# A decoder trunk on one core: other filling rates in both attentions, a later high part in the FFN, quarters for four weights, and other first and last instructions

## The chip, the cores and the metric

One core of a Trainium2 chip. The metric is device microseconds of one execution. The profile is of one execution on the same core; its times count from the span's start. A tile is [partitions, elements], 128 partitions at most.

## What is computed

A trunk of two layers on 256 tokens, width 1024, all in float32:

```python
# layer 0 (A): h = rmsnorm(x); q, k, v = h @ w_qkv_a; rope on 16 of 64 dims; 16 heads, causal (one block of 256)
x = x + attention(q, k, v) @ w_o_a
x = x + conv_ffn(rmsnorm(x))          # width 2816
# layer 1 (B): k, v = rmsnorm(x) @ w_kv_b (4 heads); q = rmsnorm(x) @ w_q_b (16 heads); rope
# window 128, a learned sink per head in the softmax
x = x + swa_sink_attention(q, k, v, sinks) @ w_o_b
x = x + conv_ffn(rmsnorm(x))
out = rmsnorm(x)

def conv_ffn(h):
    u = h @ w_up                                   # [256, 5632]
    u = conv_b + sum(conv_w[j] * shifted(u, j))    # causal, 3 taps
    gate, val = split(u)
    return (silu(gate) * val) @ w_down
```

## The kernel before

**Numbers.** Each operand of a projection is split into a high and a low part (a value rounded to the matmul's fp32r type, and the rest), and a product is three matmuls: high x high, high x low, low x high. Weights come by DMA in units of 128 x 2048 (`fetch`, three raw tiles), ScalarE makes the high part (`wh`, line 157), VectorE the low part (`wl`, line 160). `prepare` (line 166) does that in halves of 1024 columns or, for the units that line 170 lists, in quarters of 512, each piece a step of a chain. Units 0 to 15 are V, Q, K and output weights of layer A, 16 to 37 the up-projection of FFN 0, 38 to 48 its down-projection, 49 and 50 K and V of B (`U_KV`), 51 to 54 its Q (`U_QB`), 55 to 58 its output weights (`U_OB`), then FFN 1.

**The order of work.** The program is written as one stream for TensorE. `tick(ns)` moves a clock of the planner by the nominal time of the matmuls just issued; `chain(key, (delay, step), ...)` queues steps of the other engines, each due its delay after the one before, and the tick that passes a due time issues the step. `require(key)` issues what is left of a chain at once. So the delays set where an instruction stands in its engine's queue, and each engine does its queue in order.

**Projections and rotation.** `qk_group(g)` projects four heads of Q and K for both blocks of 128 tokens. `rotate` (line 371) then copies the result from PSUM, applies the rope (`rope`, lines 346 to 352, VectorE) and transposes (`to_feature`, line 358, TensorE; copies in line 364 on VectorE and 369 on ScalarE). For the first group both blocks are projected in turn and rotated at the end; behind it on TensorE come the second group's matmuls.

**Attention** (line 378) goes over four groups of four heads: scores of group g+1 (lines 402 to 409; two tiles in PSUM tag "u", one in "acc" or "t"), softmax (masks in line 422 on VectorE, exponentials in 432 on ScalarE, norms in 441 to 450), transposition of the probabilities (`probs_T`, line 461: TensorE in 463, copies to SBUF in 469 on ScalarE and 471 on VectorE), then `values` of group g (line 486), whose output gets its high part in line 492 (ScalarE) and its low part in 493 (VectorE). Between these, `fill(ns)` issues matmuls of a filler for the given nominal time: the projections of the next groups and, at the end, the output projection (`Down`, lines 533 to 538). `lead` is the time filled ahead of the first scores; `rate` gives three times for a group: ahead of its first and its second transposition, and ahead of the next scores. PSUM has four banks of tag "acc", two of "t" and two of "u".

**FFN** (line 608): for each of 22 units of 256 columns, 48 matmuls (lines 627 to 629) into a bank of "t" or "u" in turn, then `post` (line 639): ScalarE's scaled copy of both halves (L660), VectorE's two taps of each half (L664, L666), the gate's Silu on ScalarE (L670), the product on GpSimd (L671), and the high (L675, ScalarE) and low part (L676, VectorE) of the product h. `tail` (line 1002) ends the last 256 columns: sums of squares, the root on GpSimd, scaling and two output transfers.

## Time and profile before

| what | value |
| --- | --- |
| median of 3 runs | 578.2 us (578.08 to 578.53) |
| the profiled execution | 578.59 us, its span 576.7 us |
| TensorE busy | 561.9 us, 97% of the span |
| VectorE busy | 429.2 us, 74% |
| ScalarE busy | 379.3 us, 66% |
| GpSimd busy | 106.3 us, 18% |
| TensorE's granted clock | full, but for the span's last slice |

A line of the profile names the line of the kernel, the engine (PE is TensorE, PEld its weight loads, DVE VectorE, ACT ScalarE, POOL GpSimd, SP the queue of most transfers), the operation and the tiles out<-in. In a timeline the number in square brackets is the engine's idle time just before the instruction, and what ended it. Matmuls overlap at their ends, so the distance of two starts is what a matmul costs; its duration is longer.

### The profile page before, as it was taken

The page shows a single profiled execution, that of the slowest core. Times are in us where ns is not written, and L with a number is a line of the kernel's source. Part 1 is how long each engine was busy: PE and PEld are TensorE (multiplying, and loading weights), DVE is VectorE, ACT ScalarE, POOL GpSimd, SP SyncE. Part 2 cuts the span into 40 slices and gives each one's busy share as a digit, 9 for nine tenths or more (in the row PEclk, how much of TensorE's full clock was granted, in tenths as well). Part 3 has the DMA queues.
Part 4 walks back from the last instruction along what each step waited for, and adds up shares of the span by engine and source line. Part 5 has one row for each costly group of instructions (what it writes and reads, how often), then busy time and mean ns, then how long its engine had stood idle before and what let it go on. Part 6 is the DMA issues. An engine that isn't in the chain of part 4 may idle for free.

```text
span 576.7 us, 10181 instructions
## 1 busy us (share of the span) xinstructions
PE 561.9 (97%) x3858; PEld 505.3 (88%) x3858; DVE 429.2 (74%) x921; ACT 379.3 (66%) x760; POOL 106.3 (18%) x124
## 2 busy tenths in 40 slices
PE   9999999999999999999999999899999999999995
PEld 7878888789999999988888987779999999988884
DVE  6698778589967777677569798779986776777714
ACT  6888777478666566566459698867655656656513
POOL 7231001011222322321002100001222232232003
PEclk9999999999999999999999999999999999999998
DMA  8964434432654454547843633232555445355701
GB/s 331 369 251 159 147 146 147 156 138 74 223 198 165 164 202 145 194 172 288 295 145 112 255 106 114 86 135 74 156 211 194 171 157 209 147 184 218 292 0 73
DMA packets 15455, 100.99 MB, mean 175 GB/s; under 512 B 1968, under 2 KB 2096, under 8 KB 3888
## 3 DMA queue, kind: packets, MB, share of 16 engines
q1 hardware_dynamic: 15120, 100.09, 48.5%
q8 instruction: 30, 0.49, 0.3%
q10 hardware_dynamic: 288, 0.26, 0.1%
q14 instruction: 17, 0.14, 0.1%
HBM read 99.30 MB, written 1.05 MB: 174 GB/s over the span
## 4 chain that ended last, share of the span: by engine, by line
PE 60%; DVE 12%; ACT 12%; POOL 6%; issue 5%; DMA 4%; POOLq 0%; SPq 0%; DVEq 0%; ACTq 0%
PE acc L533 9%; PE acc L534 9%; PE acc L538 9%; POOL m L671 5%; DVE m L666 4%; ACT m L660 3%; DVE m L664 3%; PE acc L317 3%; PE acc L318 3%; PE acc L319 3%; DMA wr<-in_w 3%; PE t L627 3%; PE t L628 3%; PE t L629 2%; DVE wl L160 2%
## 5 line engine op out<-in xcount | busy, mean ns | idle before, releaser
L160 DVE TENSOR_TENSOR wl<-wr,wh 128x1024 fp32r<-128x1024 f32 (+1 forms) x200 | 219.2, 1114 | 32.2 <-ACT wh L157 30.3
L157 ACT ACTIVATE wh<-wr 128x1024 fp32r<-128x1024 f32 (+1 forms) x200 | 188.8, 975 | 31.2 <-PE acc L538 19.8
L671 POOL TENSOR_TENSOR m<-m,m 128x256 f32<-128x256 f32 x44 | 66.4, 1510 | 206.7 <-DVE m L666 179.8
L533 PE MATMUL acc<-wh,q 128*128 128x512 f32 x238 | 94.4, 397 | 3.1 <-ACT q L492 3.1
L534 PE MATMUL acc<-wl,q 128*128 128x512 f32 x238 | 92.9, 390 | 0.0
L627 PE MATMUL u<-q,wh 128*128 128x256 f32 x320 | 88.6, 277 | 0.7 <-DVE m L666 0.7
L628 PE MATMUL u<-q,wh 128*128 128x256 f32 x320 | 88.8, 278 | 0.0
L629 PE MATMUL u<-q,wl 128*128 128x256 f32 x320 | 88.1, 275 | 0.0
L627 PE MATMUL t<-q,wh 128*128 128x256 f32 x288 | 79.6, 276 | 0.7 <-DVE m L666 0.7
L628 PE MATMUL t<-q,wh 128*128 128x256 f32 x288 | 79.3, 275 | 0.0
L629 PE MATMUL t<-q,wl 128*128 128x256 f32 x288 | 79.2, 275 | 0.0
L538 PE MATMUL acc<-wh,q 128*128 128x512 f32 x238 | 77.2, 390 | 0.0
L675 ACT ACTIVATE q<-m 128x256 fp32r<-128x256 f32 x44 | 18.4, 418 | 85.9 <-POOL m L671 85.9
L627 PEld LDWEIGHTS u<-q,wh 128*128 128x128 f32 x320 | 60.1, 188 | 1.3 <-ACT wh L157 1.0
L628 PEld LDWEIGHTS u<-q,wh 128*128 128x128 f32 x320 | 60.1, 188 | 0.1
L629 PEld LDWEIGHTS u<-q,wl 128*128 128x128 f32 x320 | 60.1, 188 | 0.0
L317 PE MATMUL acc<-wh,q 128*128 128x512 f32 (+1 forms) x160 | 57.0, 356 | 0.0
L533 PEld LDWEIGHTS acc<-wh,q 128*128 128x128 f32 x238 | 44.7, 188 | 12.6 <-ACT q L492 3.9
L318 PE MATMUL acc<-wl,q 128*128 128x512 f32 (+1 forms) x160 | 55.6, 347 | 0.0
L319 PE MATMUL acc<-wh,q 128*128 128x512 f32 (+1 forms) x160 | 55.4, 346 | 0.0
L627 PEld LDWEIGHTS t<-q,wh 128*128 128x128 f32 x288 | 54.1, 188 | 1.2 <-ACT wh L157 0.5
L628 PEld LDWEIGHTS t<-q,wh 128*128 128x128 f32 x288 | 54.1, 188 | 0.0
(166 smaller groups left out, 1036.7 us busy)
## 6 DMA issues: line engine op xcount, KB each, us to landing
wr<-in_w SPq DMA_DIRECT2D x90, 1024.0 KB, 4.8
first<-in_xw SPq DMA_DIRECT2D x5, 384.0 KB, 5.5
xr<-in_x SPq DMA_DIRECT2D x2, 512.0 KB, 8.2
first<-in_xw SPq DMA_DIRECT2D x1, 768.0 KB, 7.0
out<-m SPq DMA_DIRECT2D x3, 256.0 KB, 2.1
fin_t<-in_fin SPq DMA_DIRECT2D x1, 512.0 KB, 5.6
first<-in_xw SPq DMA_DIRECT2D x1, 388.0 KB, 3.5
out<-m ACTq DMA_DIRECT2D x1, 256.0 KB, 2.1
```

The lines of the kernel that those rows point to most:

```text
L157: nc.scalar.activation(wq[i][0][:, c], raws[i][:, c], AF.Copy)
L160: nc.vector.tensor_tensor(out=wq[i][1][:, c], in0=raws[i][:, c], in1=f(wq[i][0][:, c]), op=ALU.subtract)
L317: nc.tensor.matmul(o, xh[:, blk(b)], wh, start=(c == 0), stop=False)
L318: nc.tensor.matmul(o, xh[:, blk(b)], wl, start=False, stop=False)
L319: nc.tensor.matmul(o, xl[:, blk(b)], wh, start=False, stop=(c == KC - 1))
L533: nc.tensor.matmul(o, ph[:, blk(b)], hi[:, s_], start=first, stop=False)
L534: nc.tensor.matmul(o, ph[:, blk(b)], lo[:, s_], start=False, stop=False)
L538: nc.tensor.matmul(o, pl[:, blk(b)], hi[:, s_], start=False, stop=end)
L627: nc.tensor.matmul(o, hi[:, s_], xh, start=(c == 0), stop=False)
L628: nc.tensor.matmul(o, hi[:, s_], xl, start=False, stop=False)
L629: nc.tensor.matmul(o, lo[:, s_], xh, start=False, stop=(c == KC - 1))
L671: nc.gpsimd.tensor_tensor(out=h, in0=gs, in1=t[1], op=ALU.mult)
```

## The change

It changes numbers that place instructions, and a few instructions:

- FFN: L675 is due 3400 ns after the gating product instead of 1200.
- Rotation of the first group: the rope is due 450 ns after the copy instead of 750, which puts it behind two quarters of a weight's low part instead of three; its transpositions stand three matmuls earlier on TensorE.
- Attention A: smaller filling times in the last group. Attention B: lead 3500 instead of 5500, and filling times by group.
- The weights of units 52 to 55 are made in quarters.
- The transposed probabilities take PSUM tag "u" instead of "t".
- Start: the copy of g moves from VectorE to GpSimd, two memsets of `kd` stand earlier on GpSimd.
- End: block 0 goes out in one transfer of 128x1024 instead of two; one product on GpSimd and one scaling of 256 columns on VectorE go, a fused product of 256 becomes one of 512; the order there is written out by hand.

```diff
--- before.py
+++ after.py
@@ -167,7 +167,7 @@
 
         if i >= N_UNITS:
             return
-        n = 4 if i <= 5 or 1 <= i - U_UP0 <= 3 or 1 <= i - U_UP1 <= 3 else 2
+        n = 4 if i <= 5 or 1 <= i - U_UP0 <= 3 or 1 <= i - U_UP1 <= 3 or U_QB + 1 <= i <= U_OB else 2
         cut = [slice(k * UNIT // n, (k + 1) * UNIT // n) for k in range(n)]
         w_time[0] = max(clock[0] + 200.0, w_time[0] + 4500.0)
 
@@ -368,11 +368,11 @@
 
         chain(key, (200.0, lambda: nc.scalar.activation(hb, v, AF.Copy)), (600.0, low))
 
-    def rotate(o, n, b, hi, lo, key, copy, then=None):
+    def rotate(o, n, b, hi, lo, key, copy, then=None, wait=750.0):
 
         t = mid()[:, :n * P]
         chain(key, (150.0, lambda: copy(t)),
-              (750.0, lambda: rope(t.rearrange("p (h d) -> p h d", d=HD), 2 * n, b)),
+              (wait, lambda: rope(t.rearrange("p (h d) -> p h d", d=HD), 2 * n, b)),
               (1000.0, lambda: to_feature(t, n, b, hi, lo, key, then)))
 
     def attention(qk, ready, filler, lead, rate, msk, vcol, sink):
@@ -458,7 +458,7 @@
             require("sm", j)
             out_ = []
             for e in range(2):
-                tp = bank("t")
+                tp = bank("u")
                 for i in range(3):
                     nc.tensor.transpose(tp[:, i * P:(i + 1) * P], pr[e][:, i * P:(i + 1) * P], ident)
                 tick(330)
@@ -672,7 +672,7 @@
 
             steps = [(200.0, scale), (700.0, tap2)] if i < n_raw else [(200.0, tap2)]
             chain(("p", i), *steps, (400.0, taps), (1600.0, gate),
-                  (1200.0, lambda: nc.scalar.activation(hi, h, AF.Copy)),
+                  (3400.0, lambda: nc.scalar.activation(hi, h, AF.Copy)),
                   (450.0, lambda: nc.vector.tensor_tensor(out=lo, in0=h, in1=f(hi), op=ALU.subtract)))
             parts.append((hi, lo))
 
@@ -747,10 +747,15 @@
         hi_part(i, c)
         lo_part(i, c)
 
+    kd = [one.tile([P, 2, 2, S], F32R, name=f"kd{i}") for i in range(2)]
+    for t in kd:
+        nc.gpsimd.memset(f(t), 0.0)
+
 
     invf = rb[:, 144:152]
     for j in range(HALF):
         nc.gpsimd.memset(invf[:, j:j + 1], float(THETA ** (-2.0 * j / ROT)))
+    nc.gpsimd.tensor_copy(g1, g0)
     pos_f = rb[:, 152:154]
     nc.gpsimd.tensor_copy(pos_f, pos_i)
     tri = rb[:, :80].rearrange("p (k b d) -> p k b d", k=5, b=NB)
@@ -775,7 +780,6 @@
         wh, wl = (t[:, (c % 4) * 512:(c % 4 + 1) * 512] for t in wq[c // 4])
         if c == 0:
             nc.vector.tensor_copy(wh, raw)
-            nc.vector.tensor_copy(g1, g0)
         nc.scalar.activation(hi, src, AF.Copy, scale=g)
         if c > 0:
             nc.scalar.activation(wh, raw, AF.Copy)
@@ -836,10 +840,6 @@
     used(0)
     used(1)
 
-    kd = [one.tile([P, 2, 2, S], F32R, name=f"kd{i}") for i in range(2)]
-    for t in kd:
-        nc.gpsimd.memset(f(t), 0.0)
-
     def spread(g, src, w):
 
         for e in range(2):
@@ -874,7 +874,7 @@
 
         def finish(b):
             rotate(o[b], 4, b, hi, lo, ("qk", g), lambda t: qk_out(t, b, o[b]),
-                   None if b else lambda src, w: spread(g, src[:, 2:4], w))
+                   None if b else lambda src, w: spread(g, src[:, 2:4], w), 750.0 if g else 450.0)
 
         gens = [proj(o[b], hT, b, cols512(u), (u, u + 1) if b else ()) for b in range(NB)]
         if g == 0:
@@ -905,7 +905,7 @@
     def ready_a(oT):
         o_down.append(Down(U_OA, 4, oT, lambda i: require("o", i)))
 
-    attention(qk, ready_a, filler_a(), 8000.0, lambda g: (7000.0, 3500.0, 2000.0) if g < 3 else (5500.0, 2500.0, 1800.0), mask, lambda h: h, False)
+    attention(qk, ready_a, filler_a(), 8000.0, lambda g: (7000.0, 3500.0, 2000.0) if g < 3 else (4500.0, 2000.0, 1500.0), mask, lambda h: h, False)
     nc.gpsimd.affine_select(out=mask[:, :P], in_=mask[:, :P], compare_op=ALU.is_gt, fill=NEG, base=0,
                             pattern=[[1, P]], channel_multiplier=-1)
 
@@ -969,7 +969,7 @@
     def ready_b(oT):
         o_down.append(Down(U_OB, 4, oT, lambda i: require("o", i)))
 
-    attention(qk, ready_b, filler_b(), 5500.0, lambda g: (3200.0, 2000.0, 1300.0), mask, lambda h: 2 * (h // 8) + h % 2, True)
+    attention(qk, ready_b, filler_b(), 3500.0, lambda g: ((4200.0, 2200.0, 1400.0), (3200.0, 1800.0, 1200.0), (3200.0, 1800.0, 1200.0), (4000.0, 1800.0, 1500.0))[g], mask, lambda h: 2 * (h // 8) + h % 2, True)
 
     hT = new_hT()
     y = [quad(F32, "y") for _ in range(2)]
@@ -994,10 +994,10 @@
         times_fin(b, half(n))
         if b == 0 and n == 1:
             r = rstd_of(b)
+            ot = spaced(qd, D, F32, "q", "ot", 15)
             for m in range(2):
-                ot = mid()
-                nc.scalar.activation(ot, xf[b][:, half(m)], AF.Copy, scale=r)
-                nc.sync.dma_start(out[:P, half(m)], ot)
+                nc.scalar.activation(ot[:, half(m)], xf[b][:, half(m)], AF.Copy, scale=r)
+            nc.sync.dma_start(out[:P], ot)
 
     def tail(m, o):
 
@@ -1009,22 +1009,24 @@
         nc.vector.tensor_tensor(out=x_, in0=o, in1=x_, op=ALU.add)
         if m == 0:
             yo.extend(mid() for _ in range(2))
-            nc.scalar.activation(yo[1][:, S:], x_, AF.Square, accum_out=st[:, 2:3])
+            nc.scalar.activation(yo[0][:, S:], x_, AF.Square, accum_out=st[:, 2:3])
             nc.scalar.activation(st[:, 1:2], st[:, 2:3], AF.Identity, scale=1.0 / D, bias=st[:, 1:2])
-            times_fin(1, c)
             return
-        nc.vector.tensor_tensor_reduce(out=xf[1][:, c], in0=x_, in1=x_, scale=1.0, scalar=0.0,
+        end = ExitStack()
+        end.enter_context(tc.manual_schedule(engines={mybir.EngineType.Activation, mybir.EngineType.DVE}))
+        nc.vector.tensor_tensor_reduce(out=yo[0][:, :S], in0=x_, in1=x_, scale=1.0, scalar=0.0,
                                        op0=ALU.mult, op1=ALU.add, accum_out=st[:, 3:4])
         nc.vector.scalar_tensor_tensor(out=st[:, 0:1], in0=st[:, 3:4], scalar=1.0 / D, in1=st[:, 1:2], op0=ALU.mult,
                                        op1=ALU.add)
         nc.gpsimd.tensor_tensor(out=r_t, in0=st[:, 0:1], in1=mhalf, op=ALU.pow)
         rows = out[P:2 * P]
+        nc.scalar.activation(yo[0][:, :S], xf[1][:, :S], AF.Copy, scale=r_t)
         nc.vector.tensor_scalar(out=yo[0][:, S:], in0=xf[1][:, S:2 * S], scalar1=r_t, scalar2=None, op0=ALU.mult)
-        nc.scalar.activation(yo[0][:, :S], xf[1][:, :S], AF.Copy, scale=r_t)
-        nc.vector.tensor_scalar(out=yo[1][:, :S], in0=xf[1][:, 2 * S:3 * S], scalar1=r_t, scalar2=None, op0=ALU.mult)
+        nc.vector.scalar_tensor_tensor(out=yo[1], in0=xr[1][:, half(1)], scalar=r_t, in1=fin_t[:, half(1)], op0=ALU.mult,
+                                       op1=ALU.mult)
         nc.scalar.dma_start(rows[:, half(0)], yo[0])
-        nc.vector.scalar_tensor_tensor(out=yo[1][:, S:], in0=x_, scalar=r_t, in1=fin_t[:, c], op0=ALU.mult, op1=ALU.mult)
         nc.sync.dma_start(rows[:, half(1)], yo[1])
+        end.close()
 
     r_t = one.tile([P, 1], F32, name="r_t")
     yo = []
```

**First place: ScalarE in the FFN.** `m` and `q` are tiles of `post`, `t` and `u` PSUM banks. Before:

```order
222 L670 ACTIVATE m_250_2353<-m_248_2351 128x256
223 L157 ACTIVATE wh_2431<-wr_2267 128x1024
224 L675 ACTIVATE q_2283<-m_251_2354 128x256
225 L660 ACTIVATE m_253_2422<-t_2355,cp 128x256
226 L660 ACTIVATE m_254_2423<-t_2355,cp 128x256
227 L157 ACTIVATE wh_2431<-wr_2267 128x1024
228 L670 ACTIVATE m_255_2424<-m_253_2422 128x256
229 L157 ACTIVATE wh_2502<-wr_2339 128x1024
230 L675 ACTIVATE q_2283<-m_256_2425 128x256
```

and now:

```order
220 L670 ACTIVATE m_250_2351<-m_248_2349 128x256
221 L157 ACTIVATE wh_2429<-wr_2266 128x1024
222 L660 ACTIVATE m_253_2420<-t_2353,cp 128x256
223 L660 ACTIVATE m_254_2421<-t_2353,cp 128x256
224 L675 ACTIVATE q_2281<-m_251_2352 128x256
225 L157 ACTIVATE wh_2429<-wr_2266 128x1024
226 L670 ACTIVATE m_255_2422<-m_253_2420 128x256
227 L157 ACTIVATE wh_2500<-wr_2338 128x1024
228 L660 ACTIVATE m_259_2492<-u_2425,cp 128x256
```

L675 of a unit (the tile `m_251`, say) stood ahead of both L660 of the next unit (`m_253`, `m_254`); now it stands behind them. The two weight halves (L157) keep their places beside L670.

**Second place: TensorE at the end of attention A.** `t` of L486 is the bank of the last values, `q_1245` and `q_1231` the tile made from it, `acc` the output projection. Before:

```order
478 L533 MATMUL acc_1021<-wh_980,q_1123 128x512
479 L534 MATMUL acc_1021<-wl_981,q_1123 128x512
480 L538 MATMUL acc_1020<-wh_980,q_1123 128x512
481 L538 MATMUL acc_1021<-wh_980,q_1123 128x512
482 L486 MATMUL t_1235<-m_123_1184,v_101 64x256
...
489 L486 MATMUL t_1235<-m_129_1219,v_102 64x128
490 L533 MATMUL acc_1018<-wh_1032,q_1245 128x512
491 L534 MATMUL acc_1018<-wl_1033,q_1245 128x512
492 L533 MATMUL acc_1020<-wh_1032,q_1245 128x512
```

and now:

```order
468 L538 MATMUL acc_1020<-wh_980,q_1123 128x512
469 L538 MATMUL acc_1021<-wh_980,q_1123 128x512
470 L486 MATMUL t_1221<-m_123_1184,v_101 64x256
...
477 L486 MATMUL t_1221<-m_129_1212,v_102 64x128
478 L533 MATMUL acc_1018<-wh_980,q_1123 128x512
479 L534 MATMUL acc_1018<-wl_981,q_1123 128x512
...
488 L538 MATMUL acc_1020<-wh_980,q_1123 128x512
489 L538 MATMUL acc_1021<-wh_980,q_1123 128x512
490 L533 MATMUL acc_1018<-wh_1032,q_1231 128x512
```

Before, the unit that reads the values' tile (`wh_1032`) came right behind the values; now 12 matmuls of the unit before it (`wh_980`) lie between.

**Third place: ScalarE in attention B, ahead of the high part of the third group's values (L492).** Before:

```order
401 L469 ACTIVATE m_422_4247<-t_4242 128x384
402 L157 ACTIVATE wh_4309<-wr_3957 128x512 x4
403 L432 ACTIVATE m_426_4279,hst_4281<-m_426_4279,hst_4281 128x128
404 L432 ACTIVATE m_427_4280,hst_4281<-m_427_4280,hst_4281 128x128
405 L432 ACTIVATE m_426_4279,hst_4281<-m_426_4279,hst_4281 128x256
406 L435 ACTIVATE hst_4281<-hst_4281,sink_t 128x2
407 L432 ACTIVATE m_427_4280,hst_4281<-m_427_4280,hst_4281 128x256
408 L492 ACTIVATE q_4300<-t_4285 128x512
```

and now:

```order
399 L157 ACTIVATE wh_4220<-wr_3874 128x1024
400 L469 ACTIVATE m_422_4256<-u_4251 128x384
401 L432 ACTIVATE m_426_4289,hst_4291<-m_426_4289,hst_4291 128x128
402 L432 ACTIVATE m_427_4290,hst_4291<-m_427_4290,hst_4291 128x128
403 L432 ACTIVATE m_429_4292,hst_4294<-m_429_4292,hst_4294 128x128
404 L432 ACTIVATE m_430_4293,hst_4294<-m_430_4293,hst_4294 128x128
405 L432 ACTIVATE m_426_4289,hst_4291<-m_426_4289,hst_4291 128x256
406 L435 ACTIVATE hst_4291<-hst_4291,sink_t 128x2
407 L432 ACTIVATE m_427_4290,hst_4291<-m_427_4290,hst_4291 128x256
408 L492 ACTIVATE q_4310<-t_4295 128x512
```

Four weight quarters stood ahead of the exponentials; now they are placed one by one behind L492.

## Rows read from the trace of the kernel before

**Rows 1.** The page: busy time of each engine with its share of the span; and from the costliest groups (count, busy us and mean ns, then idle time ahead of them and what ended it) the line of L675.

```profile
PE 561.9 (97%) x3858; PEld 505.3 (88%) x3858; DVE 429.2 (74%) x921; ACT 379.3 (66%) x760; POOL 106.3 (18%) x124
...
L675 ACT ACTIVATE q<-m 128x256 fp32r<-128x256 f32 x44 | 18.4, 418 | 85.9 <-POOL m L671 85.9
```

**Rows 2.** Windows of five stages: start and end, length, then busy us (and instructions) of each engine, TensorE's clock, the share of the DMA engines and GB/s.

```profile
60.00:110.00 50.00, 50.00 (x287) 40.83 (x287) 33.98 (x101) 35.49 (x87) 2.65 (x5) 1.00 0.44 153
...
200.00:250.00 50.00, 49.31 (x395) 47.51 (x395) 36.59 (x57) 29.21 (x48) 14.02 (x9) 1.00 0.49 173
...
300.00:320.00 20.00, 19.34 (x108) 16.17 (x108) 19.89 (x51) 18.62 (x46) 5.67 (x6) 1.00 0.40 138
320.00:370.00 50.00, 48.35 (x381) 42.02 (x379) 40.85 (x163) 41.63 (x120) 0.00 (x0) 1.00 0.38 135
370.00:400.00 30.00, 28.30 (x193) 24.60 (x194) 23.38 (x65) 21.47 (x59) 1.73 (x2) 1.00 0.31 107
```

**Rows 3.** Waits of TensorE: who waited for whom, us in total, times, longest.

```profile
PE acc L533 <- ACT q L492: 3.1, 3, 1.6
PE t L358 <- DVE m L352: 1.4, 3, 0.6
...
PE u L627 <- DVE m L666: 0.7, 2, 0.3
PE t L627 <- DVE m L666: 0.7, 2, 0.3
```

**Rows 4.** TensorE's timeline in FFN 0: the first matmul of a unit and of the next one (start, us, instruction).

```profile
213.31 0.28 PE L627 MATMUL t<-q,wh 128*128 128x256 f32 x1
...
218.75 0.28 PE L627 MATMUL u<-q,wh 128*128 128x256 f32 x1
```

**Rows 5.** The chain that ended last, in FFN 0: start, us, what. One turn of the ring.

```profile
224.31 1.57 POOL m L671
...
225.91 0.42 ACT q L675
226.32 0.92 ACT m L660 x2
...
227.27 0.49 DVE m L664
...
227.79 0.48 DVE m L666
...
229.71 0.48 DVE m L666
...
230.35 1.57 POOL m L671
```

**Rows 6.** Groups by line and shape: the low part of a weight, by its two widths, and the low part of h.

```profile
L160 DVE TENSOR_TENSOR wl<-wr,wh 128x1024 fp32r<-128x1024 f32 x160 | 193.2, 1221 | 23.7 <-ACT wh L157 23.4
...
L160 DVE TENSOR_TENSOR wl<-wr,wh 128x512 fp32r<-128x512 f32 x40 | 26.1, 685 | 8.4 <-ACT wh L157 7.0 <-PE acc L319 1.5
...
L676 DVE TENSOR_TENSOR q<-m,q 128x256 fp32r<-128x256 f32 x44 | 18.8, 428 | 43.4 <-ACT q L675 43.4
```

**Rows 7.** The first rotation: VectorE's timeline, then TensorE's.

```profile
27.57 1.30 DVE L160 TENSOR_TENSOR wl<-wr,wh 128x512 fp32r<-128x512 f32 x2 [1.48 <-PE acc L319]
29.76 0.69 DVE L160 TENSOR_TENSOR wl<-wr,wh 128x512 fp32r<-128x512 f32 x1 [0.90 <-ACT wh L157]
30.37 0.28 DVE L346 TENSOR_TENSOR rb<-m,cs 128x128 f32<-128x128 f32 x1
...
30.58 0.39 PE L319 MATMUL acc<-wh,q 128*128 128x512 f32 x1
31.40 0.63 PE L358 MATMUL t<-ident,m 128*128 128x128 f32 x4 [0.43 <-DVE m L352]
32.32 0.63 PE L358 MATMUL t<-ident,m 128*128 128x128 f32 x4 [0.30 <-DVE m L352]
```

**Rows 8.** The end of attention A: TensorE's timeline, then ScalarE's.

```profile
109.44 1.52 PE L486 MATMUL t<-m,v 128*64 128x256 f32 x16
111.75 0.50 PE L533 MATMUL acc<-wh,q 128*128 128x512 f32 x1 [0.79 <-ACT q L492]
...
109.55 1.67 ACT L157 ACTIVATE wh<-wr 128x512 fp32r<-128x512 f32 x3 [2.25 <-PE acc L538]
```

**Rows 9.** K, V, Q and attention B: TensorE's timeline where it waited, then ScalarE's ahead of the longest wait.

```profile
319.16 0.41 PE L358 MATMUL t<-ident,m 128*128 128x128 f32 x2 [0.64 <-DVE m L352]
...
335.00 0.44 PE L463 MATMUL t<-ident,m 128*128 128x128 f32 x2 [0.20 <-ACT m L448]
...
370.41 0.50 PE L533 MATMUL acc<-wh,q 128*128 128x512 f32 x1 [1.64 <-ACT q L492]
...
377.78 1.52 PE L486 MATMUL t<-m,v 128*64 128x256 f32 x16 [0.32 <-DVE m L471]
380.00 0.49 PE L533 MATMUL acc<-wh,q 128*128 128x512 f32 x1 [0.70 <-ACT q L492]
...
365.74 2.20 ACT L157 ACTIVATE wh<-wr 128x512 fp32r<-128x512 f32 x4 [0.88 <-PE acc L538]
```

**Rows 10.** The end: the timeline of all engines, the GpSimd product and the VectorE instruction beside it.

```profile
570.34 0.72 POOL L990 TENSOR_TENSOR xf<-xr,fin_t 128x256 f32<-128x256 f32 x1 [0.65 <-DVE xr L1009]
...
570.68 0.66 DVE L1016 CUSTOM_DVE_ANT_0 xf<-xr 128x256 f32<-128x256 f32 x1
```

## Prediction

> **What bounds the kernel now.** I read the profile in this order: the page's busy times, the windows by stage, TensorE's waits, and then the timelines of the places where TensorE is not full. TensorE is busy for 97% of the span, no other engine for more than 74% (its weight loads aside) [rows 1]. So what VectorE, ScalarE or GpSimd does costs time only where TensorE waits for it, and a change of order can win at most the 3% that is left. The windows say where these lie [rows 2]: 60 to 110 us is 50.00 of 50; 0.69 is lost from 200 to 250 (the end of FFN 0's up-projections), 0.66 from 300 to 320 (K and V), 1.65 and 1.70 from 320 to 400 (Q and attention B). From 300 to 320 VectorE is busy for 19.89 of 20 us and ScalarE for 18.62: there the helpers are the limit. TensorE's waits name the partners [rows 3]: ScalarE's high part of the attention output (L492), 3.1 us in three waits; the rope's last step (L352), 1.4 in three; the conv taps (L666), 0.7 + 0.7 in four. Idle time understates a stall a little, since the first matmul behind it runs longer, so where I can I count from start to start. A unit of 48 matmuls of 128x256 takes 5.44 us (213.31 to 218.75), 0.113 each [rows 4]; one of 128x512 twice that, and I count 0.11 for a transposition.
>
> **FFN: the high part of h gets a delay of 3400 instead of 1200.** The chain that ended last repeats a ring every 6.04 us, from one gating product on GpSimd (224.31) to the next (230.35) [rows 5]: the product 1.57, its high part L675 0.42 on ScalarE, both L660 of the next unit 0.92, VectorE's L664 0.49, then 1.92 for L666, L664 and a weight's low part (227.79 to 229.71), L666 0.48, and 0.15 to the next product (some 0.1 of hand-overs beside). ScalarE works in order: L660 of the next unit stands behind L675, which waits for GpSimd, 85.9 us in all [rows 1]. TensorE's unit of 5.44 is 0.60 shorter than the ring. Four PSUM banks hide that for a while; then TensorE pays it unit by unit, which is the four waits for L666, two in each FFN: 4 x 0.60 = 2.4. The unit before each pair pays a part; I take 0.15 each. In the change, L675 of a unit stands behind L660 of the next one. The ring is then the product 1.57, L675 0.45 with its hand-over, L676 0.43 [rows 6], 1.92, 0.48 and 0.15: 5.0 us. That is 0.44 under TensorE's 5.44, so the waits go. **2.7 us**; 0 if the ring turns out 0.44 or more longer than I add up.
>
> **First rotation (750 to 450).** VectorE makes three quarters of a weight's low part ahead of the first rope, and the third waits for ScalarE until 29.76, so the rope runs from 30.37. TensorE's two groups of transpositions start at 31.40 and 32.32 [rows 7]: 0.82 after the matmul at 30.58 where 0.23 would do, and 0.92 after the first group where 4 x 0.11 would do: 1.07 lost. Now two quarters stand ahead of the rope, which end at 28.87, and the transpositions come three matmuls (0.68) earlier. A rope takes about 0.92 (the step from 31.40 to 32.32), so the first is through near 29.9, ahead of the 30.1 at which TensorE gets there (30.58 + 0.23 - 0.68), and the second near 30.8, some 0.2 late. **0.85 us** (0.6 to 1.07).
>
> **End of attention A (rates of the last group).** Behind the last values (109.44) the unit that reads them begins at 111.75, 0.79 idle and a slow start: 0.85; ScalarE had three weight quarters (1.67 us) to do before L492 [rows 8]. With the smaller rates the values come earlier, and 12 down matmuls (2.7 us) stand between them and their reader. Even with the three quarters first and 0.6 for L492, 2.3, that covers it. **0.85 us**, less only if the transpositions of probabilities, now 6 matmuls earlier, find theirs not ready (0.3 at worst, half of the 1.36 by which they move up being slack).
>
> **K, V, Q and attention B (rates, lead, quarters of units 52 to 55, the banks).** The large stalls are 0.64 idle at 319.16, 0.20 at 335.00, 1.64 at 370.41, 0.32 at 377.78 and 0.70 at 380.00, 3.5 in sum [rows 9]. At 370.41 TensorE waits for L492, and ScalarE did four weight quarters (365.74, 2.20 us) before the exponentials that stand ahead of L492. Now six matmuls (1.36) stand between values and reader, and no four quarters ahead of the exponentials: 0.2 stays, 1.45 won. The 0.20 (transposition waits for the normed probabilities, L448) goes, since the first scores are issued earlier (lead 3500, and a first rate of 4200 instead of 3200). The 0.32 waits for the copy L471, behind which the values' bank comes free; with the transposed probabilities in the other tag it goes. Of the 0.64 only 0.05 is won, as VectorE has no gap there; the 0.70 stays. Three slow starts go with their stalls, 0.4. That is 2.4. Against it stand the quarters: eight instructions more on VectorE and eight on ScalarE. By mean durations one more costs 2 x 0.685 - 1.221 = 0.15 of VectorE [rows 6]; but two in a row take 1.30 [rows 7], not 1.37, so 0.08: 0.6 to 1.2 us more, where VectorE has none to spare. I charge 0.4, since much of it falls where VectorE has room (370 to 400: 23.38 of 30). **2.0 us**, from -0.5 (only half of the big stall goes, and the quarters cost 1.2) to 3.3 (no charge, and the 0.64 goes too with its slow start).
>
> The Trainium skill speaks against the quarters: "VectorE: DVE Perf Modes", § "The TRN2 errata — SBUF-src ops pay a fixed extra latency per instruction", gives about 150 fixed cycles an instruction, by my estimate from it 0.157 us, 1.26 for eight; and "Perfetto Trace Analysis", § "Optimizing Scalar/DVE Operations", wants fewer, larger operations on a saturated engine. By that rule the term would be 1.1 and the time 572.5. The rows agree with 0.15 as a duration, but show 0.08 where two follow each other.
>
> **Both ends.** At the start a copy leaves VectorE and two memsets move on GpSimd; TensorE's waits name neither: 0.05 (0 to 0.3). At the end, GpSimd's product (570.34, 0.72) beside VectorE's L1016 (570.68, 0.66) is gone [rows 10]; if half of their overlap (0.38) was contention, 0.15 to 0.2. The last VectorE work keeps its 768 columns, in two instructions instead of three, with the second transfer still behind both: 0. **0.15** (-0.2 to 0.4). The output of block 0 in one transfer instead of two lies beside matmuls: 0.
>
> **Sum.** 2.7 + 0.85 + 0.85 + 2.0 + 0.05 + 0.15 = 6.6 us. The profiled execution took 578.59 us, 0.39 more than the median of 578.2: 572.0 for such a one, **571.6** for the median.
>
> **Rivals.** (1) The FFN ring stays at 5.44 or above. For it: the product takes 1.57 on GpSimd only because a weight's low part runs beside it (the one at the end takes 0.72 for the same tile [rows 10]), so another place of the weights can lengthen the ring. Against it: 0.44 of room. 2.7 lost: 574.3. (2) In B the helpers are the limit and the stalls only move: the term is 0, 573.6. For it: 19.89 of 20. Against it: the largest stall lies at 370, where VectorE is at 78%, and comes from order. (3) Slower: the transposed probabilities take the two banks of the scores. TensorE can't write the next scores before both copies are out, nor transpose before VectorE's masking has read both scores, and a copy or a mask can stand behind a weight half of 1.22. With one such wait of 1.1 in each of the eight groups, and B's 2.0 gone, it is 578.2 - 4.6 + 8.8 = 582.4; it decides from 0.58 a group on. Against it: at 335.00 the transposition waited for L448, which comes behind the masks anyway. (4) The won time comes back as waits for weights: 578, no change. Against it: TensorE's wait rows name no transfer.
>
> **Chances.** Forecast 0.58, rival 1 0.13, rival 2 0.19, rival 3 0.05, rival 4 0.05. A measurement of this kernel can tell 0.2%, 1.2 us, from no change. Forecast and rivals 1 and 2 are faster by more: 0.90; same 0.05; slower 0.05. The range reaches from 569.5 (B at 3.3, both ends and the rotation at their best, and 0.1) to 575.5 (rival 1 with half of rival 2).
>
> **What would show it.** No TensorE wait for L666, and the products 5.44 apart, with L675's idle time far under 85.9. Waits for L492 near 1 us instead of 3.1. The transpositions behind the first rope at most 0.3 late. Wrong would be waits of L409 or L463 for L469, L471 or L422 above 0.5 each, or a loss from 60 to 110.

## The result

The changed kernel takes 570.8 us in the median of four runs (570.39 to 571.34), against 578.14 before: 7.3 us less, a ratio of 0.9873 (95% interval 0.9856 to 0.989). Forecast were 571.6 in 569.5 to 575.5. The profiled execution took 570.39 us, its span 568.3; the one before 578.59 and 576.7, so the two traces differ by 8.4 us of span, 1.1 more than the medians. Line numbers of the changed kernel are up to 5 higher between lines 750 and 840 and the same again behind that (L990 is still the product with the final gain), but for the last lines: L1017 is what was L1016.

Where the time went is read from the starts of the same TensorE instruction in both timelines:

| first matmul of | before | after | difference | won in the stage |
| --- | --- | --- | --- | --- |
| Q and K of the first group | 16.52 | 16.41 | -0.11 | start 0.1 |
| scores of the first group (L409) | 39.49 | 38.27 | -1.22 | first rotation 1.1 |
| FFN 0, up | 118.67 | 116.43 | -2.24 | attention A 1.0 |
| FFN 0, down | 241.92 | 237.96 | -3.96 | FFN 0 1.7 |
| K and V | 303.27 | 299.31 | -3.96 | 0 |
| FFN 1, up | 386.82 | 380.15 | -6.67 | attention B 2.7 |
| FFN 1, down | 510.16 | 502.08 | -8.08 | FFN 1 1.4 |
| (last matmul) | 569.91 | 561.83 | -8.08 | 0 |

Another 0.3 is won behind the last matmul. What TensorE waits for, the answer to [rows 3]:

```profile
PE acc L533 <- ACT q L492: 0.7, 1, 0.7
PE t L715 <- DVE m L719: 0.6, 2, 0.3
PE t L358 <- DVE m L352: 0.4, 1, 0.4
PE acc L739 <- ACT q L783: 0.4, 1, 0.4
```

The two names of L666 are gone, the three waits for L492 have become one (0.7). Of the rope's three none is left; the one of 0.4 is new. The wait of L739 lies at the start and comes and goes between the traces of kernels with the same start. The windows that answer to [rows 2] (columns as there):

```profile
60.00:110.00 50.00, 50.00 (x292) 40.92 (x291) 33.41 (x94) 34.52 (x84) 2.62 (x5) 1.00 0.41 148
...
200.00:250.00 50.00, 50.00 (x391) 47.92 (x390) 39.37 (x62) 32.99 (x54) 8.35 (x9) 1.00 0.58 203
...
300.00:320.00 20.00, 19.96 (x127) 17.50 (x126) 19.26 (x55) 17.78 (x45) 6.80 (x6) 1.00 0.53 191
320.00:370.00 50.00, 49.43 (x372) 42.62 (x371) 42.82 (x167) 43.60 (x133) 0.00 (x0) 1.00 0.32 114
370.00:400.00 30.00, 29.04 (x223) 26.30 (x222) 25.86 (x61) 22.39 (x51) 3.32 (x4) 1.00 0.34 119
```

From 200 to 250 nothing is lost, from 300 to 320 0.04 instead of 0.66 though VectorE is still 96% busy, from 320 to 400 1.5 instead of 3.35.

**The ring** [rows 5]. GpSimd's timeline in FFN 0, VectorE's low part of a weight beside two of the products, then ScalarE's of one turn:

```profile
202.02 1.56 POOL L671 TENSOR_TENSOR m<-m,m 128x256 f32<-128x256 f32 x1 [3.39 <-ACT m L660]
206.97 1.56 POOL L671 TENSOR_TENSOR m<-m,m 128x256 f32<-128x256 f32 x1 [3.39 <-ACT m L660]
211.92 0.75 POOL L671 TENSOR_TENSOR m<-m,m 128x256 f32<-128x256 f32 x1 [3.39 <-ACT wh L157]
...
206.72 1.21 DVE L160 TENSOR_TENSOR wl<-wr,wh 128x1024 fp32r<-128x1024 f32 x1
...
211.94 1.80 DVE L160 TENSOR_TENSOR wl<-wr,wh 128x1024 fp32r<-128x1024 f32 x1 [0.19 <-ACT wh L157]
...
201.31 1.01 ACT L660 ACTIVATE m<-u,cp 128x256 f32<-128x256 f32 x2
203.62 0.42 ACT L675 ACTIVATE q<-m 128x256 fp32r<-128x256 f32 x1 [1.30 <-POOL m L671]
```

The products are 4.95 us apart up to 211.92 (5.0 was added up), then 5.03 to 5.28, and 5.44 from 227.26 on: there the ring has caught up with TensorE, so the 5.44 that the prediction named as a sign comes only at the end. The product at 211.92 takes 0.75 instead of 1.56; it begins 0.02 us ahead of the low part beside it, which takes 1.80 instead of 1.21. ScalarE does both L660 ahead of L675, and L675's idle time is 40.2 us instead of 85.9.

**The first rotation** [rows 7], VectorE, then TensorE: the rope runs from 27.59, right behind the quarters of the weight, and the transpositions don't wait.

```profile
27.59 0.29 DVE L346 TENSOR_TENSOR rb<-m,cs 128x128 f32<-128x128 f32 x1
...
29.78 0.39 PE L319 MATMUL acc<-wh,q 128*128 128x512 f32 x1
30.01 1.03 PE L358 MATMUL t<-ident,m 128*128 128x128 f32 x8
```

**The end of attention A** [rows 8] and **attention B** [rows 9], TensorE:

```profile
105.30 1.52 PE L486 MATMUL t<-m,v 128*64 128x256 f32 x16
106.75 0.50 PE L533 MATMUL acc<-wh,q 128*128 128x512 f32 x1
...
336.51 0.44 PE L358 MATMUL t<-ident,m 128*128 128x128 f32 x2 [0.42 <-DVE m L352]
...
373.33 0.50 PE L533 MATMUL acc<-wh,q 128*128 128x512 f32 x1 [0.69 <-ACT q L492]
```

Behind the values of attention A the down matmuls go on without a gap (106.75, 1.45 us after the values began). In B a wait for a rope costs 0.42 at 336.51, which was not there before, and the last L492 still 0.69 at 373.33; the stall of 1.64 has no successor.

**The end** [rows 10]: without GpSimd's product beside it, the same sum of squares takes 0.42 instead of 0.66.

```profile
562.60 0.42 DVE L1017 CUSTOM_DVE_ANT_0 m<-xr 128x256 f32<-128x256 f32 x1
```

### The profile page after: what moved, and what is told of

The parts are those of the page before. It is cut to its first block, busy times and chain, and to the rows that moved or that the text cites. A ratio compares the mean times of both kernels' runs of the same rounds, so it can differ in the third digit from the quotient of the medians.

```text
span 568.3 us, 10191 instructions
## 1 busy us (share of the span) xinstructions
PE 558.8 (98%) x3858; PEld 504.5 (89%) x3858; DVE 427.1 (75%) x927; ACT 380.0 (67%) x768; POOL 100.3 (18%) x124
## 4 chain that ended last, share of the span: by engine, by line
PE 88%; DVE 5%; ACT 4%; issue 1%; POOL 1%; DMA 1%; DVEq 0%; POOLq 0%; ACTq 0%
PE acc L533 9%; PE acc L538 9%; PE acc L534 9%; PE u L628 6%; PE u L629 6%; PE u L627 6%; PE t L628 6%; PE t L629 6%; PE t L627 6%; PE acc L317 4%; PE acc L319 4%; PE acc L318 4%; PE acc L739 2%; PE acc L628 2%; PE acc L629 2%; PE acc L627 2%
## 5 line engine op out<-in xcount | busy, mean ns | idle before, releaser
L157 ACT ACTIVATE wh<-wr 128x1024 fp32r<-128x1024 f32 (+1 forms) x208 | 190.0, 946 | 75.0 <-PE acc L538 55.4
L671 POOL TENSOR_TENSOR m<-m,m 128x256 f32<-128x256 f32 x44 | 60.2, 1367 | 182.2 <-DVE m L666 109.2
L629 PEld LDWEIGHTS t<-q,wl 128*128 128x128 f32 x288 | 54.1, 188 | 0.0
```

Of the source, the lines that this page charges most:

```text
L157: nc.scalar.activation(wq[i][0][:, c], raws[i][:, c], AF.Copy)
L629: nc.tensor.matmul(o, lo[:, s_], xh, start=False, stop=(c == KC - 1))
L671: nc.gpsimd.tensor_tensor(out=h, in0=gs, in1=t[1], op=ALU.mult)
```

## The experiments

All were timed against the kernel before, on the same chip as the others of their set.

### Parts alone

The FFN delay alone:

```diff
-                  (1200.0, lambda: nc.scalar.activation(hi, h, AF.Copy)),
+                  (3400.0, lambda: nc.scalar.activation(hi, h, AF.Copy)),
```

> The kernel before with the delay of L675 at 3400 and nothing else. My theory (the ring falls from 6.04 to about 5.0 us, under TensorE's 5.44): no wait of TensorE for L666, 2.7 to 3.2 us faster than before, 575.0 to 575.5. Rival 1 (the ring stays at 5.44 or above, and what FFN won in the whole change came from somewhere else): 0 to 0.5 us faster, 577.6 to 578.2.

Measured: 575.31 against 578.11, ratio 0.9953 (0.9941 to 0.9966), 2.8 us. No wait for L666 is left, and the products stand 4.95 apart:

```profile
198.47 1.57 POOL L671 TENSOR_TENSOR m<-m,m 128x256 f32<-128x256 f32 x1 [3.39 <-DVE m L666]
203.42 1.57 POOL L671 TENSOR_TENSOR m<-m,m 128x256 f32<-128x256 f32 x1 [3.39 <-ACT m L660]
```

The theory holds, in size too: 2.7 was the term.

The first rotation alone:

```diff
-              (750.0, lambda: rope(t.rearrange("p (h d) -> p h d", d=HD), 2 * n, b)),
+              (wait, lambda: rope(t.rearrange("p (h d) -> p h d", d=HD), 2 * n, b)),
...
-                   None if b else lambda src, w: spread(g, src[:, 2:4], w))
+                   None if b else lambda src, w: spread(g, src[:, 2:4], w), 750.0 if g else 450.0)
```

> The kernel before with the rope of the first group due after 450 instead of 750. My theory (third quarter ahead of the rope was the stall): the two waits of 0.43 and 0.30 go, 0.85 to 1.1 us faster, 577.0 to 577.3. Rival (the scores behind it then wait for the copies of the transposed tile): under 0.3 us faster.

Measured: 577.81 against 578.11, ratio 0.9992 (0.9983 to 1.0), so 0.3 us, at most 1.0. In its trace the two waits are gone and the first scores are 1.3 us earlier than in the trace before (1.2 in the whole change). But the trace before is one execution, and its stall was a large one. In the trace of the run with the FFN delay alone, with the rotation as before, the transpositions start at 30.79 without a wait of TensorE in the list. What differs is when the weight arrives. ScalarE's timeline ahead of the rotation, before:

```profile
26.90 1.16 ACT L157 ACTIVATE wh<-wr 128x512 fp32r<-128x512 f32 x2 [1.78 <-DMA wr<-in_w]
```

and with the FFN delay alone:

```profile
25.69 1.16 ACT L157 ACTIVATE wh<-wr 128x512 fp32r<-128x512 f32 x2 [0.57 <-DMA wr<-in_w]
```

The same two quarters wait 1.78 us for the transfer in one and 0.57 in the other; the run with attention A's rates alone has 1.28, and its transpositions start at 31.11. The traces of the other kernels with the old place show how much hangs on it. From the first matmul of Q and K to the first scores (L409) they take 22.97 us (wait 1.78, the trace before), 22.58 (1.28), 22.07 (0.83, the run of attention B alone) and 22.04 (0.57). With the rope at 450 it is 21.85 to 21.95 in every trace, also where that wait is 1.21 (this run) or 1.41 (the changed kernel once more). So with the edit the late arrival no longer reaches TensorE, and it wins 1.1 where the transfer is as late as in the trace before, 0.2 where it is early. These are four executions; how often a transfer is late is not known. The gain that this trace has is not lost again in FFN 0, whose up-projection lasts 123.25 us as before.

The smaller rates of attention A alone:

```diff
-(5500.0, 2500.0, 1800.0)
+(4500.0, 2000.0, 1500.0)
```

> The kernel before with the smaller filling times in the last group of attention A, transposed probabilities still in tag t. My theory (12 down matmuls cover the high part L492): 0.85 to 1.0 us faster, 577.1 to 577.3. Rival (transpositions or values come too early and wait for the softmax, or need the other bank): under 0.3 us faster.

Measured: 578.73 against 578.11, ratio 1.0011 (1.0002 to 1.0019): 0.6 us slower. Both forecasts of the time were wrong. The wait behind the values is gone as expected (its FFN 0 begins at 117.59 instead of 118.67; 0.8 of this lies in attention A), but FFN 0's up-projection ends at 241.98, where it ended before (241.92). TensorE's waits:

```profile
PE t L627 <- DVE m L666: 1.2, 4, 0.3
...
PE u L627 <- DVE m L666: 1.0, 3, 0.3
```

Seven waits for L666 instead of four, 2.2 us instead of 1.4. GpSimd's products and a piece of ScalarE's queue in this run:

```profile
142.68 2.67 POOL L671 TENSOR_TENSOR m<-m,m 128x256 f32<-128x256 f32 x1 [6.00 <-ACT m L670]
150.24 2.62 POOL L671 TENSOR_TENSOR m<-m,m 128x256 f32<-128x256 f32 x1 [4.89 <-ACT m L670]
...
163.94 1.56 POOL L671 TENSOR_TENSOR m<-m,m 128x256 f32<-128x256 f32 x1 [4.03 <-DVE m L666]
...
145.39 0.42 ACT L675 ACTIVATE q<-m 128x256 fp32r<-128x256 f32 x1 [2.78 <-POOL m L671]
145.71 2.00 ACT L157 ACTIVATE wh<-wr 128x1024 fp32r<-128x1024 f32 x2
```

The same before:

```profile
146.29 0.75 POOL L671 TENSOR_TENSOR m<-m,m 128x256 f32<-128x256 f32 x1 [7.62 <-DVE m L666]
150.28 1.48 POOL L671 TENSOR_TENSOR m<-m,m 128x256 f32<-128x256 f32 x1 [3.25 <-ACT m L670]
...
163.86 1.56 POOL L671 TENSOR_TENSOR m<-m,m 128x256 f32<-128x256 f32 x1 [4.48 <-DVE m L666]
...
144.64 1.99 ACT L157 ACTIVATE wh<-wr 128x1024 fp32r<-128x1024 f32 x2
147.07 0.42 ACT L675 ACTIVATE q<-m 128x256 fp32r<-128x256 f32 x1 [0.44 <-POOL m L671]
```

And in the run of the first rotation alone:

```profile
162.53 1.56 POOL L671 TENSOR_TENSOR m<-m,m 128x256 f32<-128x256 f32 x1 [4.48 <-DVE m L666]
```

From 163.94 and 163.86 on the ring turns every 6.04 us. It is not in step earlier although TensorE began FFN 0 1.08 us earlier, and what TensorE gained it waited for later. A slow ring does not by itself take away what is won ahead of it: with the first rotation alone FFN 0 begins 1.34 us earlier than before (117.33), the ring of 6.04 is in step 1.33 earlier (162.53), and the up-projection ends 1.33 earlier (240.59). There ScalarE, VectorE and GpSimd do the work of FFN 0 in the order of before. With the smaller rates the order in its first units is another: L675 comes ahead of two weight halves instead of behind them, and the third and fourth products take 2.67 and 2.62 us, beside two low parts of weights each, instead of 0.75 and 1.48. The third begins 3.6 us earlier than before, the fourth at the same time. That the rates change this order and that the ring is late behind it is shown; which of the moved steps makes it late was not tried. To see whether the loss depends on the delay of L675, the same edit was taken out of the whole change:

```diff
-(4500.0, 2000.0, 1500.0)
+(5500.0, 2500.0, 1800.0)
```

> The changed kernel with attention A's filling times as before. My theory now (what the smaller times win in attention A was lost again in FFN 0 of the run with them alone, because the ring of 6.04 us there ended when it ended; with the ring at 4.95 it is kept): 0.8 to 1.0 us slower than the changed kernel, 571.6 to 571.8, 6.3 to 6.5 faster than before. Rival (the smaller times cost something of their own in FFN 0, whatever the ring): the same as the changed kernel or up to 0.6 faster.

Measured: 571.9, ratio 0.9895 (0.988 to 0.991) to the kernel before; the whole change has 0.9873, and in another set 0.988. That is 0.9 to 1.3 us slower by the ratios, so with the later L675 attention A's gain is kept. By the traces 0.8 of it lies in attention A and 0.3 in FFN 0, whose up-projection takes 121.53 us with the smaller times and 121.87 without; with the old delay it took 124.39 with them and 123.25 without. The rival (a cost whatever the ring) falls. The theory's number came, but its reason, that a ring of 6.04 ends when it ends, is not shown: with the first rotation alone such a ring ended earlier.

Attention B alone (lead and rates, quarters, banks):

```diff
-U_UP1 <= 3 else 2
+U_UP1 <= 3 or U_QB + 1 <= i <= U_OB else 2
...
-                tp = bank("t")
+                tp = bank("u")
...
-filler_b(), 5500.0, lambda g: (3200.0, 2000.0, 1300.0),
+filler_b(), 3500.0, lambda g: ((4200.0, 2200.0, 1400.0), (3200.0, 1800.0, 1200.0), (3200.0, 1800.0, 1200.0), (4000.0, 1800.0, 1500.0))[g],
```

> The kernel before with what the change does to attention B: lead and filling times, quarters of units 52 to 55, transposed probabilities in tag u (that in attention A too). My theory (order is at fault, not the helpers' throughput): 2.0 to 2.7 us faster, 575.4 to 576.1, waits for L492 at about 1.5 instead of 3.1. Rival 2 (VectorE and ScalarE are the limit, stalls move): 0 to 0.5 us faster. The Trainium skill's rule on small operations: about 1.1 us faster.

Measured: 575.2 against 578.11, ratio 0.9949 (0.9935 to 0.9963), 2.9 us; its waits for L492 are 1.5 us in two. By the traces some 0.3 of it lies in attention A, where the banks are changed too, and 2.4 from K and V to FFN 1. Rival 2 falls.

### Attention B taken apart

Three kernels, each the changed one with one part as before. Quarters undone:

```diff
-U_UP1 <= 3 or U_QB + 1 <= i <= U_OB else 2
+U_UP1 <= 3 else 2
```

> The changed kernel with the weights of units 52 to 55 in halves again. The prediction (quarters cost 0.4 of the term): 0.4 us faster than the changed kernel, 570.4. The Trainium skill's rule on fixed cost per instruction: 1.2 faster, 569.6. Rival, from the trace after (the wait at the rope of K shrank from 0.64 to 0.2 as its last step stands behind a quarter of 0.68 instead of a half of 1.21): 0.3 to 0.8 slower, 571.1 to 571.6.

Measured: 571.02, ratio 0.9878 (0.9862 to 0.9895). By time that is the changed kernel within 0.3 us; by the traces the stretch from K and V to FFN 1 takes 0.6 us more (299.68 to 381.14, against 299.31 to 380.15). VectorE's timeline at the rope of K, then TensorE's:

```profile
313.86 1.21 DVE L160 TENSOR_TENSOR wl<-wr,wh 128x1024 fp32r<-128x1024 f32 x1
315.00 0.41 DVE L352 TENSOR_TENSOR m<-rb 128x64 f32<-128x64 f32 x1
...
315.56 0.41 PE L358 MATMUL t<-ident,m 128*128 128x128 f32 x2 [0.63 <-DVE m L352]
```

The rope's last step (L352) stands behind a half of 1.21 us again, and TensorE waits 0.63, as at 319.16 before [rows 9]; with quarters it stands behind 0.68, and TensorE's wait is too short to be listed. So quarters don't cost 0.4 there, they cost nothing and win up to 0.6, in spite of eight more instructions on a full engine: what TensorE waits for is not the engine's sum of work but the piece that lies ahead of the one it needs. The Trainium skill's rule ("VectorE: DVE Perf Modes", § "The TRN2 errata — SBUF-src ops pay a fixed extra latency per instruction") would have had 1.2 won by halves, by the estimate that the prediction made from it; no run shows that. Another page of the Trainium skill has the sentence that fits, "Perfetto Trace Analysis", § "Optimizing Scalar/DVE Operations": breaking up instructions may let work that others wait for end sooner. It limits that to engines that aren't saturated, and here it held on one that is 96% busy.

Banks undone:

```diff
-                tp = bank("u")
+                tp = bank("t")
```

> The changed kernel with the transposed probabilities in tag t again. The prediction (the values' bank waits for a copy): 0.3 to 0.9 us slower than the changed kernel, 571.1 to 571.7, with a wait of values (L486) for L471. Rival (that wait went because of the filling times): no difference within 0.3.

Measured: 571.86, ratio 0.9893 (0.9878 to 0.9908), 0.8 to 1.2 us slower than the changed kernel. TensorE's waits:

```profile
PE t L486 <- DVE m L471: 0.5, 1, 0.5
...
PE t L463 <- DVE m L471: 0.2, 1, 0.2
```

Values wait for the copy L471 once more. The prediction holds, at about three times the size it gave (0.32): with tag t there are also a wait of the transposition for that copy and, by the traces, 0.2 us in attention A, where the tag is undone too. The rival falls.

Lead and rates undone:

```diff
-filler_b(), 3500.0, lambda g: ((4200.0, 2200.0, 1400.0), (3200.0, 1800.0, 1200.0), (3200.0, 1800.0, 1200.0), (4000.0, 1800.0, 1500.0))[g],
+filler_b(), 5500.0, lambda g: (3200.0, 2000.0, 1300.0),
```

> The changed kernel with attention B's lead and filling times as before (5500; 3200, 2000, 1300), quarters and banks as changed. The prediction (order is what stalled TensorE): the wait of 1.6 for L492 and the 0.45 at the first probabilities come back, 1.5 to 2.4 us slower than the changed kernel, 572.3 to 573.2. Rival 2 (the helpers' throughput is the limit): under 0.5 slower. Rival 3's mechanism (scores and transposed probabilities share banks) would show as waits of L409 or L463 for L469 or L471, 3 or more slower.

Measured: 573.01, ratio 0.9915 (0.9901 to 0.993), 2.0 to 2.4 us slower than the changed kernel. TensorE's and ScalarE's timelines:

```profile
366.10 0.49 PE L533 MATMUL acc<-wh,q 128*128 128x512 f32 x1 [1.64 <-ACT q L492]
...
361.43 2.20 ACT L157 ACTIVATE wh<-wr 128x512 fp32r<-128x512 f32 x4 [0.88 <-PE acc L538]
```

It is the stall of before, to the hundredth: four quarters (2.20 us) ahead of the exponentials and 1.64 of idle time at the reader. No wait of scores or transpositions for a copy shows here or in the changed kernel, so rival 3 never came up.

### The ring made longer

```diff
                 nc.gpsimd.tensor_tensor(out=h, in0=gs, in1=t[1], op=ALU.mult)
+                nc.gpsimd.tensor_tensor(out=h, in0=gs, in1=t[1], op=ALU.mult)
```

> The changed kernel with the gating product issued twice in a row on GpSimd (the same result). The ring of 4.95 us gets 0.75 longer if the second one runs alone, 1.57 if a weight's low part runs beside it too. The prediction's condition (the waits come back when the ring is 0.44 longer): waits of TensorE for L666, some us slower than the changed kernel. My theory now: before, some 14 units ran at 6.04 against 5.44, 8.4 us of lag, and only 1.35 of it became waits, so each FFN hides about 7 us of lag; the waits come back only from a ring of 5.44 + 7/14 = 5.94 on. At 5.7 no loss at all, at 6.5 about 8 us for each FFN, 16 us slower.

Measured: 574.95, ratio 0.9946 (0.9932 to 0.9961), 3.8 us slower than the changed kernel in the same set (571.11). GpSimd's timeline, then TensorE's at the first matmul of a unit:

```profile
165.82 1.59 POOL L671 TENSOR_TENSOR m<-m,m 128x256 f32<-128x256 f32 x1 [3.36 <-DVE m L666]
...
212.01 1.59 POOL L671 TENSOR_TENSOR m<-m,m 128x256 f32<-128x256 f32 x1 [3.36 <-DVE m L666]
213.68 0.74 POOL L672 TENSOR_TENSOR m<-m,m 128x256 f32<-128x256 f32 x1
217.78 1.58 POOL L671 TENSOR_TENSOR m<-m,m 128x256 f32<-128x256 f32 x1 [3.36 <-DVE m L666]
...
167.66 0.28 PE L627 MATMUL t<-q,wh 128*128 128x256 f32 x1
...
211.66 0.28 PE L629 MATMUL u<-q,wl 128*128 128x256 f32 x1
212.01 0.36 PE L627 MATMUL t<-q,wh 128*128 128x256 f32 x1
...
217.78 0.36 PE L627 MATMUL u<-q,wh 128*128 128x256 f32 x1
```

The second product takes 0.74 and the ring 5.77. TensorE is in step with it: 212.01 to 217.78 is 5.77 too, 0.33 more than 5.44, and so for six units from 200.47 to 235.09. FFN 0's up-projection takes 2.3 us more than in the changed kernel (123.80 against 121.53), FFN 1's 2.0. So the prediction's condition was right (a ring more than 0.44 longer costs), and the later theory, that 7 us of lag are hidden, fell: it took what was hidden before the change for a constant. What is hidden is the head start that the ring has when it gets into step. Once TensorE waits for it, a product and a unit begin together (217.78). Nine turns back the product at 165.82 belongs to the unit at 167.66, so the head start is 1.84 us, and about six turns of 0.33 use it up. Before, a product and a unit begin together at 224.3, and ten turns back the product at 163.86 belongs to a unit that begins at 169.79: 5.93 us, for ten turns of 0.60. By the same count it is 4.46 with attention A's smaller rates alone and 5.96 with the first rotation alone, and the one pays for more units than before, the other for as many. Each of these waits leaves under 0.1 us of idle time in the profile, since a matmul's end overlaps the next one; the list of TensorE's waits doesn't name L666 at all, and only the starts show it (211.66 and 0.28 make 211.94, and the next begins at 212.01).

### Two versions that go further

The last wait for L492 in B (0.69) can be covered as in attention A, with six matmuls behind the last values. The first run is the changed kernel once more, the others are two ways to get those six.

> The changed kernel itself, to compare the next two with on the same chip: 570.4 to 571.4.

> The changed kernel with the last group's filling times of attention B at 4000, 900, 1 instead of 4000, 1800, 1500: six matmuls move from between the last two transpositions to behind the last values. My theory (L492 is covered by those six, 1.36 us, as in attention A): the wait of 0.69 at 373.33 goes, 0.5 to 0.8 us faster than the changed kernel, 570.0 to 570.3. Rival (the transposition then waits for the norm L448 or the values for the copies L469 and L471): within 0.2.

```diff
-(4000.0, 1800.0, 1500.0))[g]
+(4000.0, 900.0, 1.0))[g]
```

> The changed kernel with attention B's lead at 2300 instead of 3500 and the last group's times at 4000, 1800, 1: the six matmuls come from ahead of the first scores. My theory: the wait of 0.69 goes here too, 0.5 to 0.8 us faster than the changed kernel, less what the first transposition waits as its scores move. Rival (the whole attention has moved ahead of its rotations, and waits for L352 take the place): no faster, or slower by up to 0.8.

```diff
-filler_b(), 3500.0,
+filler_b(), 2300.0,
...
-(4000.0, 1800.0, 1500.0))[g]
+(4000.0, 1800.0, 1.0))[g]
```

Measured against 578.08: 571.11 (ratio 0.988, 0.9864 to 0.9897), 569.69 (0.9859, 0.9845 to 0.9874) and 569.21 (0.9847, 0.9832 to 0.9861): 1.4 and 1.9 us below the changed kernel, more than expected. One of the four runs of the first took 571.22, and the profiled executions (570.74, 569.74 and 569.30) lie 1.0 and 1.4 apart, so the medians may say a little too much. TensorE's waits in the last one, and its timeline at the end of attention B:

```profile
PE u L251 <- DVE warm L227: 1.1, 1, 1.1
PE t L715 <- DVE m L719: 0.6, 2, 0.3
...
369.64 1.52 PE L486 MATMUL t<-m,v 128*64 128x256 f32 x16
371.09 0.50 PE L533 MATMUL acc<-wh,q 128*128 128x512 f32 x1
```

Neither L492 nor L352 is among the waits (in the first version 0.2 is left for L492), and matmuls follow the last values without a gap. By the traces the first of the two wins 0.6 in attention B and the second 1.1 (with lead 2300 the rope's wait of 0.42 goes too, against the rival), and both 0.4 in FFN 1, whose first units TensorE does in another order than in the changed kernel. FFN 0 of the changed kernel has that order too, with attention A's smaller rates, and there it comes with the 0.3 named above. No expectation had this, and its cause was not tried.

## Why the prediction was right, and where it was off

The forecast of 6.6 us was 0.7 short of the 7.3 measured, and the forecast case is the one that came. That the sum comes so near is in part luck: the first rotation was taken too large and attention B too small.

- **FFN, 2.7.** 2.8 alone, by the traces 1.4 in each FFN. The ring of 5.0 is 4.95, and its threshold was tested from the other side. The prediction let the banks hide the lag "for a while"; what hides it is the ring's head start, 5.93 us before.
- **First rotation, 0.85.** 0.3 alone (0 to 1.0), and 0.2, 0.2, 0.7 and 1.1 against the four traces with the old place. This term was mis-sized: it counted the stall of one execution whole. The row that warned stood in the trace: ScalarE's two quarters ahead of it had waited 1.78 us for a transfer. The prediction followed the chain back from TensorE to VectorE and to ScalarE, and stopped one step short of the transfer.
- **End of attention A, 0.85.** 0.9 to 1.3 within the change, and -0.6 alone. In attention A itself it was right (0.8 by the traces). What the prediction left out is that the filling times also move what the helpers do in the first units of FFN 0: with the old delay of L675 that costs 1.1, with the new one 0.3 is won. So it is not a term that can be added up by itself.
- **Attention B, 2.0.** 2.9 alone, 2.7 by the traces. Rates and lead (2.0 to 2.4) carry most of it, as the prediction had it for the stall at 370.41. The charge of 0.4 for the quarters had the wrong sign: of the 0.64 at the rope of K the prediction gave 0.05, since VectorE has no gap there, and with quarters most of it went. The banks are worth 0.8 to 1.2 rather than 0.32. By the traces the three parts, undone one at a time, come to 2.2, 1.3 and 0.6 in B, more than the 2.7 together, so they overlap.
- **Both ends, 0.2.** By the traces 0.3 at the end: from the start of the last matmul it takes 6.43 to 6.45 us in every trace with the new end and 6.77 to 7.18 in those with the old one. The 0.1 at the start is not shown, as the first matmul of Q and K begins at 16.30 to 16.79 in the traces with the old start and at 16.41 to 16.83 in those with the new one. Both are too small for a run by itself, and none was made.

Rival 1 fell with the run of the FFN alone, rival 2 with that of attention B alone; rival 3 needs waits that no run with the probabilities in tag u has; of rival 4 there is no sign. The upper end of the range was added up as 575.5, where its own terms (574.3 and half of 2.0) give 575.3.

## What to carry to other kernels

Where one engine is nearly full, list its stalls with what ended each, and follow each one back until nothing waits; the last step (a transfer here) says whether the stall belongs to the order or to that execution. Before adding up gains, ask what an edit moves further on: numbers that place instructions by a planner's clock also change the order behind the place they are meant for, and one edit can win with a second one and lose without it. Where a loop of helpers is slower than the engine it feeds, measure its head start when it gets into step; that says for how many turns it stays hidden. On a full helper engine the size of the piece ahead of the awaited instruction can matter more than the sum of work.

## What the runs showed of the hardware

A 128x256 float32 product on GpSimd takes 0.74 to 0.75 us alone and 1.56 beside a weight's low part on VectorE that began ahead of it (206.97 and 206.72 in the changed kernel). Where the product began first, by 0.02 us (211.92), it took 0.75 and the low part 1.80 instead of 1.21. VectorE's sum of squares took 0.66 beside such a product and 0.42 without. The Trainium skill has the two engines contend for SBUF where a VectorE instruction has two inputs there ("GPSIMD Engine Reference", § "8. Key points"); the trace agrees, since a low part reads `wr` and `wh`, and the sum of squares its tile twice. A stall of TensorE of 0.33 us at each unit left no entry among its waits, in the kernel with the second product.
